# Weights of the stationary-slot products: the low part of every second half built as minus the high part plus the weights, by an accumulating transfer

## The chip, the cores and the metric

One core of one Trainium2 chip runs the whole program. The metric is the device time of one execution, in microseconds (us). Two times stand side by side in the texts: the span of a profiled execution, from its first instruction to its last, and the median of unprofiled runs.

## The reference, cut to what matters

```python
def swiglu(x, w_gate, w_up, w_down):
    return (jax.nn.silu(x @ w_gate) * (x @ w_up)) @ w_down
...
        f = swiglu(rms_norm(h, ffn1_pre_g[i]), ffn1_w_gate[i], ffn1_w_up[i], ffn1_w_down[i])
        h = h + 0.5 * rms_norm(f, ffn1_post_g[i])
        u = rms_norm(h, mix_pre_g[i])
        proj = u @ w_in[i]
...
        merged = g[:, :, 0] * (o_att @ w_branch_att[i]) + g[:, :, 1] * (o_ssm @ w_branch_ssm[i])
        h = h + rms_norm(merged @ w_out[i], mix_post_g[i])
        f = swiglu(rms_norm(h, ffn2_pre_g[i]), ffn2_w_gate[i], ffn2_w_up[i], ffn2_w_down[i])
        h = h + 0.5 * rms_norm(f, ffn2_post_g[i])
```

A decoder layer of width 2048 on 256 tokens in float32: a SwiGLU feed-forward (inner width 5632), then differential attention and a Mamba-2 mixer side by side, then a second feed-forward. Nearly all of the arithmetic is in products of 256 tokens with large float32 weight matrices.

## The kernel before, in words

**Exact products out of two parts.** A float32 number is split into a high part, rounded to the short float32r format (`hi`), and the rest (`lo`). A large product is the sum of hi\*hi, hi\*lo and lo\*hi, gathered in PSUM by TensorE. The tokens' side stands on chip as "slots", already split. The weights stream through the chip once, and every piece is split on arrival.

**Two forms of product.** `project_t` (lines 162 to 177) makes its result [feature, token], with the weights stationary. `project` (lines 121 to 149) makes it [token, feature], with the slots stationary and the weights moving. The change touches `project` alone. It serves the down projections of both feed-forwards (88 chunks), the v, z and gate columns of `w_in` (80), `w_ssm` (32), `w_att` (16) and `w_out` (16): 232 chunks of 1 MB, [128, 4, 512] in float32.

**How one chunk goes through `project`.** SyncE (SP) loads it into a buffer `raw`, of which there are 3 (line 131). It is worked off in two halves of [128, 2, 512]. For each half `split` (lines 102 to 113) takes a `hi` and a `lo` tile out of rings of 4 each, ScalarE (ACT) writes `hi` (line 111) and VectorE (DVE) writes `lo` = `raw` - `hi` (line 112). TensorE (PE) then runs 12 matmuls of 512 columns on the half: for each of two blocks and two token tiles one with `hi` (line 117), one with `lo` (line 118), and one with `hi` again (line 119). A half's `hi` and `lo` go back to their rings when its matmuls are done, and the half four places on takes them. Both kinds of product share the rings.

**Late chunks.** With `by_token=2` (three products: the last slab of each feed-forward and of `w_out`) the last two chunks are held and gone through once per token tile, so four halves stand in the rings at once.

**What sets the order.** Each engine works through its own instructions in one fixed order; a scheduler sets it when the program is built. GpSimd (POOL) does the elementwise multiplications behind `project_t` (lines 304, 306, 386), the decay matrices of the Mamba-2 groups (a DMA into `dec` at line 503, and after DVE's line 505 and ACT's line 507 a multiplication at line 512), small powers (lines 95, 274), and issues a few DMAs. It touches no weights. A list `queue` puts the first splits of a product behind chosen instructions; each call of `split` takes one entry of it.

Of the kernel before, what the change touches and what calls it, by code (L numbers as in the profile page):

```python
"""Macaron SwiGLU pair around differential attention and a Mamba-2 mixer, on one core.

The operand x of a large product stands on chip as "slots" [feature, token], 512 features each. A
float32 operand is the exact sum of two float32r parts (hi = rounded to 12 significant bits, lo =
the rest), and a large product is hi*hi + hi*lo + lo*hi accumulated in PSUM. Weights stream through
SBUF once. A product comes out as [token, feature] (slots stationary, `project`) or, where its
transpose is what is needed next, as [feature, token] (weights stationary, `project_t`).
"""
# [9 lines left out]
F32 = mybir.dt.float32  # L18
F32R = mybir.dt.float32r
AF = mybir.ActivationFunctionType  # L20
ALU = mybir.AluOpType
# [5 lines left out]
NT = 2  # token tiles  # L27
S = 512  # columns of a slab
# [4 lines left out]
# columns of the packed per-partition vectors  # L33
# [3 lines left out]
# slabs of w_in, and of its columns that come out transposed  # L37
# [5 lines left out]
def decoder_layer(ctx: ExitStack, tc: tile.TileContext, x, x_t, cols, rows, post_g, wg1, wu1, wd1, w_in,  # L43
# [15 lines left out]
    # ---- constants  # L59
    ident = const.tile([P, P], F32, name="ident")  # L60
    make_identity(nc, ident)
    tri = const.tile([P, P], F32, name="tri")  # 1 where row <= column
# [3 lines left out]
    neg = const.tile([P, P], F32, name="neg")  # 0 where column <= row, else -1e30  # L66
# [11 lines left out]
    raw0 = raws.tile([P, 8, 256], F32, name="raw")  # the first weights, between the pieces of x  # L78
# [4 lines left out]
    row = const.tile([P, 192], F32, name="row")  # dt_bias | a_log | d, on every partition  # L83
    nc.gpsimd.dma_start(row, rows.partition_broadcast(P))

    def bc(ap, n):
        """[P, k] -> [P, k, n], each element repeated n times."""
        return ap.unsqueeze(2).broadcast_to([P, ap.shape[1], n])

    def rsqrt(dst, ss, n):  # L90
        """dst = (ss / n + eps) ** -0.5"""
        k = ss.shape[1]
        v = small.tile([P, 2], F32, name="rs_v")
        nc.vector.tensor_scalar(v[:, :k], ss, 1.0 / n, EPS, ALU.mult, ALU.add)
        nc.gpsimd.tensor_tensor(out=dst, in0=v[:, :k], in1=mhalf[:, :k], op=ALU.pow)

    loaded = [None]
    queue = []  # instructions that the next splits are issued behind
# [15 lines left out]

    def matmul3(ps, sl, j, t, wh, wl, first, last):
        xh, xl = (sl[:, j, i, t * P:(t + 1) * P] for i in range(2))
        nc.tensor.matmul(ps, xh, wh, start=first, stop=False)  # L117
        nc.tensor.matmul(ps, xh, wl, start=False, stop=False)  # L118
        nc.tensor.matmul(ps, xl, wh, start=False, stop=last)  # L119

    def project(xs, w, n, by_token=0):
        """xs: slots over the contraction; w(n, c): [P, 4, S], the chunk of slot c. -> PSUM [P, NT, S].
        by_token: the last so many chunks are taken token tile by token tile, to have the first of
        them early. -> two PSUM tiles [P, S]."""
        ps = ([psm.tile([P, S], F32, name="acc_t", tag="m") for _ in range(NT)] if by_token else
              acc.tile([P, NT, S], F32, name="acc"))
        at = lambda t: ps[t] if by_token else ps[:, t]
        tail = []
        for c, sl in enumerate(xs):
            raw = raws.tile([P, 4, S], F32, name="raw")  # L130
            nc.sync.dma_start(raw, w(n, c))
            for b in range(2):
                hi, lo = split(raw[:, 2 * b:2 * b + 2], [P, 2, S])
                for jj in range(2):
                    j = 2 * b + jj
                    tail.append((sl, j, hi[:, jj], lo[:, jj], c + j == 0, c == len(xs) - 1 and j == 3))
            if c < len(xs) - by_token:
                for sl_, j, wh, wl, first, last in tail:
                    for t in range(NT):
                        matmul3(at(t), sl_, j, t, wh, wl, first, last)  # L140
                tail = []
        for t in range(NT):
            for sl_, j, wh, wl, first, last in tail:
                matmul3(at(t), sl_, j, t, wh, wl, first, last)
        return ps
# [17 lines left out]
    def project_t(xs, *products, raw=None, before=None):  # L163
        """products: (w, n) each, chunk by chunk in turn; w(n, c): [P, 8, 256], the chunk of slots 2c and
        2c + 1. -> SBUF [feature, 2, token] of each. raw: the first chunk, loaded already;
        before(b, js): what makes the blocks js of slot b."""
        ps = [acc.tile([P, 2, 2 * TT], F32, name="acc") for _ in products]  # hi*hi | hi*lo + lo*hi
        for c in range(len(xs) // 2):
            for i, (w, n) in enumerate(products):
                first = i == 0 and c == 0  # L170
                chunk_t(ps[i], xs, w, n, c, raw if first else None, before if i == 0 else None)
        out = []
        for p in ps:
            out.append(tmp.tile([P, 2, TT], F32, name="pt", tag="t2"))
            nc.scalar.activation(out[-1], p[:, :, TT:], AF.Copy)  # L175
            nc.vector.tensor_tensor(out=out[-1], in0=p[:, :, :TT], in1=out[-1], op=ALU.add)  # L176
        return out
# [4 lines left out]
    def fill(sl, j, src):  # L182
        """Parts of src [P, k, TT] into the slot's blocks j, j + 1, ..."""
        js = slice(j, j + src.shape[1])
        nc.scalar.activation(sl[:, js, 0], src, AF.Copy)
        nc.vector.tensor_tensor(out=sl[:, js, 1], in0=src, in1=sl[:, js, 0].bitcast(F32), op=ALU.subtract)

    def fill_gain(sl, j0, src, gain):
        """The same of src times gain, which has a column for each block of the slot."""
# [7 lines left out]
    def to_slot(src, gain=None):  # L197
        """src: two [P, S] tiles by token -> slot, times gain [P, 4] by feature."""
# [13 lines left out]
    def pre_slots(gain, update):  # L212
        """Slots of h * gain; update(c) brings piece c of h's second token tile up to date."""
        xs = []
        for c in range(4):
            u = update(c)
            if c == 0:
                queue.extend([(), (), (u,), (u,)])
            xs.append(to_slot([h[t][:, c * S:(c + 1) * S] for t in range(NT)], col[:, gain + 4 * c:gain + 4 * c + 4]))
        return xs  # L220

    def pre_scale():
        """The tokens' 1/rms of h, to be applied to the products: [P, NT] by token, and [P, TT] along
        the free axis."""
# [9 lines left out]
    def spread(s1):  # L234
        """Sums of squares by token, [P, NT] -> the pair that pre_scale gives."""
# [11 lines left out]
    class PostNorm:  # L247
        """h += scale * rms_norm(f) * g, f given slab by slab."""
# [6 lines left out]
        def slab(self, n, get):  # L255
# [7 lines left out]
            if n == 2:  # k * (sum of squares / D + eps), but for the last slab's squares  # L263
# [4 lines left out]
        def finish(self):  # L268
            """Brings h of the first token tile up to date. -> what does so for piece c of the second."""
# [64 lines left out]
    # ======== FFN 1  # L334
    xs = [new_slot() for _ in range(4)]

    def scale1():
        """pre_scale of x, from its transpose."""
# [21 lines left out]
    # ======== token mixers  # L360
# [7 lines left out]
    # Work between two products whose steps wait for each other is a generator; one step of it is  # L368
    # issued behind each of the large products.
# [20 lines left out]
    # ---- dt, decays  # L390
# [19 lines left out]
    # softplus(v) = max(v, 0) + 2 atanh(e / (2 + e)), e = exp(-|v|)  # L410
# [10 lines left out]
    nc.vector.tensor_tensor(out=e, in0=e, in1=q, op=ALU.mult)  # z, at most 1/3  # L421
    nc.vector.tensor_tensor(out=q, in0=e, in1=e, op=ALU.mult)  # z * z
# [11 lines left out]
    acs = const.tile([P, NT, 64], F32, name="acs")  # cumulated in each chunk (= token tile)  # L434
# [3 lines left out]
    dend = const.tile([P, 64], F32, name="dend")  # exp(last - acs), first chunk  # L438
    nc.vector.tensor_tensor(out=dend, in0=ptot, in1=acs[:, 0], op=ALU.subtract)
    nc.scalar.activation(dend, dend, AF.Exp)  # L440
    din = const.tile([P, 64], F32, name="din")  # exp(acs), second chunk
# [10 lines left out]
    # ---- lambda  # L452
# [15 lines left out]
    def conv_silu(halves, blocks):  # L468
        """halves: w_in_t slabs; blocks: the conv's 128-channel block of each quarter.
        -> silu(conv) as [channel, block, token]."""  # L470
# [15 lines left out]
    def ssd_group(g, xc, bct, zs):  # L486
        """One group's 8 heads: 512 channels. Appends its slot to done."""
# [3 lines left out]
        xv = hpool.tile([P, 4, S], F32, name="xv", tag="h")  # x*dt of both chunks, x*D of both  # L491
# [7 lines left out]
        # decay between positions of a chunk, [s, head, l]  # L499
# [30 lines left out]
        # the first chunk's state, seen by the second  # L530
# [10 lines left out]
        # gate and group norm  # L541
# [11 lines left out]
    part = big.tile([P, NT, D], F32, name="part", tag="big")  # the ssm branch, then the merge  # L553
# [34 lines left out]
    # ---- attention, two heads a slab  # L588
# [20 lines left out]
    def softmax_av(qT, kT, vs, wait):  # L609
        o, pr, dT = [], {}, {}  # L610

        def probs(hh):
            """Difference of the two maps' softmax, by query."""
# [97 lines left out]
    # ======== FFN 2  # L711
# [54 lines left out]
```

## Time and profile before

| | |
|---|---|
| median of 3 runs | 2865.27 us (2863.51 to 2866.38) |
| span of the profiled execution | 2861.1 us |
| instructions | 36115 |
| bytes moved by DMA | 537.44 MB, 188 GB/s on average |
| granted TensorE clock, mean | 0.997 of full speed (2.4 GHz) |

The profiled execution has no device time of its own beside its span; the median of the runs lies 4.2 us above the span. The busy shares of the engines are averages over the whole program. What decides in a stage is which wait ends last there, so the order of the views is: busy shares, then the chain of waits that ended last, then the instructions of one stage in order of time.

### The profile page before, as it was taken

How to read it: one execution, taken by the hardware profiler on the slowest of the kernel's cores; microseconds unless marked ns; L12 is line 12 of the kernel's file. 1: busy time of each engine (PE TensorE's matmuls, PEld its weight loads, DVE VectorE, ACT ScalarE, POOL GpSimd, SP SyncE). 2: the span in 40 equal slices, each digit the busy share in tenths (PEclk: the TensorE clock that was granted, in tenths of full speed). 3: DMA queues.
4: the chain of work that ended last, by engine and by line, in shares of the span. 5: the costliest groups of instructions: out<-in, count | busy, mean ns of one | idle time of the engine just before them, and what ended most of it. 6: DMA issues, size and time to landing. Idle time of an engine off the chain costs nothing.

```text
span 2861.1 us, 36115 instructions
## 1 busy us (share of the span) xinstructions
PE 2823.8 (99%) x14540; PEld 2398.2 (84%) x14540; DVE 1707.9 (60%) x2018; ACT 1374.3 (48%) x1695; POOL 285.8 (10%) x219
## 2 busy tenths in 40 slices
PE   8999999999999999999999999999999999999998
PEld 7888888888788888888788888888878888888887
DVE  6554555555678776777765555545556545554555
ACT  5444444444555555545444444444455444443443
POOL 1100110011012210112100000000001100110110
PEclk9999999999999999999999999999999999999999
DMA  6565555556554555545554545555545555555554
GB/s 238 188 219 190 186 190 191 192 186 200 192 198 168 179 189 179 189 162 192 205 182 171 177 167 185 199 191 184 195 171 180 191 192 189 191 183 197 183 195 155
DMA packets 77127, 537.44 MB, mean 188 GB/s; under 512 B 8672, under 2 KB 8816, under 8 KB 13728
## 3 DMA queue, kind: packets, MB, share of 16 engines
q1 hardware_dynamic: 73152, 521.17, 53.2%
q0 software_dynamic: 3664, 13.80, 1.5%
q8 instruction: 114, 1.87, 0.3%
q14 instruction: 53, 0.43, 0.0%
q10 hardware_dynamic: 144, 0.17, 0.0%
HBM read 530.84 MB, written 4.26 MB: 187 GB/s over the span
## 4 chain that ended last, share of the span: by engine, by line
PE 91%; issue 4%; DVE 3%; DMA 0%; ACT 0%; POOL 0%; SPq 0%; DVEq 0%; POOLq 0%; ACTq 0%
PE acc L159 33%; PE acc L160 17%; PE acc L118 13%; PE acc L119 13%; PE acc L117 13%; PE pyd L525 1%; DVE w_lo L112 1%; PE tp L205 1%; PE sc L618 0%; PE po L646 0%; DVE dec L505 0%; DVE xc L480 0%; DMA xT<-in_x_t 0%; PE pyo L537 0%; PE pst L532 0%
## 5 line engine op out<-in xcount | busy, mean ns | idle before, releaser
L112 DVE TENSOR_TENSOR w_lo<-raw,w_hi 128x1024 fp32r<-128x1024 f32 (+1 forms) x979 | 1245.8, 1276 | 1028.9 <-ACT w_hi L111 1026.7
L111 ACT ACTIVATE w_hi<-raw 128x1024 fp32r<-128x1024 f32 (+1 forms) x979 | 1034.5, 1059 | 1249.5 <-PE acc L159 631.1
L159 PE MATMUL acc<-slot,w_hi 128*128 128x512 f32 x4096 | 1448.8, 399 | 8.5 <-DVE slot L193 7.1
L160 PE MATMUL acc<-slot,w_lo 128*128 128x256 f32 x4096 | 1148.5, 280 | 0.5 <-DVE w_lo L112 0.5
L159 PEld LDWEIGHTS acc<-slot,w_hi 128*128 128x128 f32 x4096 | 770.3, 188 | 194.4 <-ACT w_hi L111 9.5
L160 PEld LDWEIGHTS acc<-slot,w_lo 128*128 128x128 f32 x4096 | 774.2, 189 | 4.0 <-DVE w_lo L112 2.3
L118 PE MATMUL acc<-w_lo,slot 128*128 128x512 f32 x1776 | 693.3, 390 | 6.0 <-DVE w_lo L112 6.0
L117 PE MATMUL acc<-w_hi,slot 128*128 128x512 f32 x1776 | 697.4, 393 | 0.0
L119 PE MATMUL acc<-w_hi,slot 128*128 128x512 f32 x1776 | 692.8, 390 | 0.0
L118 PEld LDWEIGHTS acc<-w_lo,slot 128*128 128x128 f32 x1776 | 334.2, 188 | 77.2 <-DVE w_lo L112 7.2
L117 PEld LDWEIGHTS acc<-w_hi,slot 128*128 128x128 f32 x1776 | 334.3, 188 | 70.5 <-issue 1.0
L119 PEld LDWEIGHTS acc<-w_hi,slot 128*128 128x128 f32 x1776 | 334.1, 188 | 69.3
L304 POOL TENSOR_TENSOR pt<-pt,rb 128x512 f32<-128x512 f32 x44 | 58.9, 1338 | 1118.4 <-DVE pt L176 1113.6
L176 DVE TENSOR_TENSOR pt<-acc,pt 128x512 f32<-128x512 f32 x128 | 87.5, 683 | 2.6 <-ACT pt L175 2.6
L175 ACT ACTIVATE pt<-acc 128x512 f32<-128x512 f32 x128 | 74.3, 580 | 1.8 <-PE acc L160 1.8
L480 DVE SCALAR_TENSOR_TENSOR xc<-pt,col,xc 128x255 f32<-128x255 f32 (+2 forms) x144 | 61.9, 482 | 14.1 <-ACT xc L477 13.9
L306 POOL TENSOR_TENSOR pt<-pt,rb 128x512 f32<-128x512 f32 x44 | 65.2, 1483 | 33.7 <-ACT pt L305 33.7
L512 POOL TENSOR_TENSOR dec<-dec,cb 128x1024 f32<-128x1024 f32 x16 | 55.8, 3504 | 121.9 <-ACT dec L507 121.9
L386 POOL TENSOR_TENSOR pt<-pt,rb 128x512 f32<-128x512 f32 x24 | 36.5, 1521 | 208.7 <-DVE pt L176 208.7
L477 ACT ACTIVATE xc<-pt,col 128x256 f32<-128x256 f32 x48 | 26.8, 594 | 40.3 <-POOL pt L386 40.3
L305 ACT ACTIVATE pt<-pt 128x512 f32<-128x512 f32 x44 | 27.9, 633 | 26.1 <-POOL pt L304 26.1
L309 DVE TENSOR_TENSOR pt<-pt 128x512 f32<-128x512 f32 x44 | 30.5, 692 | 7.5 <-POOL pt L306 3.1
(195 smaller groups left out, 1034.8 us busy)
## 6 DMA issues: line engine op xcount, KB each, us to landing
raw<-in_wu SPq DMA_DIRECT2D x88, 1024.0 KB, 4.8
raw<-in_wd SPq DMA_DIRECT2D x88, 1024.0 KB, 4.9
raw<-in_wg SPq DMA_DIRECT2D x87, 1024.0 KB, 4.9
raw<-in_w_in SPq DMA_DIRECT2D x80, 1024.0 KB, 4.8
raw<-in_w_in_t SPq DMA_DIRECT2D x80, 1024.0 KB, 4.9
raw<-in_w_ssm SPq DMA_DIRECT2D x32, 1024.0 KB, 4.8
raw<-in_w_att SPq DMA_DIRECT2D x16, 1024.0 KB, 4.8
raw<-in_w_out SPq DMA_DIRECT2D x16, 1024.0 KB, 4.8
```

Source lines behind the costliest of these rows:

```text
L111: nc.scalar.activation(hi[:, js], raw[:, js], AF.Copy)
L112: nc.vector.tensor_tensor(out=lo[:, js], in0=raw[:, js], in1=hi[:, js].bitcast(F32), op=ALU.subtract)
L117: nc.tensor.matmul(ps, xh, wh, start=first, stop=False)
L118: nc.tensor.matmul(ps, xh, wl, start=False, stop=False)
L119: nc.tensor.matmul(ps, xl, wh, start=False, stop=last)
L159: nc.tensor.matmul(ps[:, f], hi[:, j, wf], sl[:, j], start=b + j == 0, stop=False)
L160: nc.tensor.matmul(ps[:, f, TT:], lo[:, j, wf], sl[:, j, :TT], start=False, stop=b == len(xs) - 1 and j == 3)
L175: nc.scalar.activation(out[-1], p[:, :, TT:], AF.Copy)
L176: nc.vector.tensor_tensor(out=out[-1], in0=p[:, :, :TT], in1=out[-1], op=ALU.add)
L304: nc.gpsimd.tensor_tensor(out=g, in0=g, in1=rb, op=ALU.mult)
L306: nc.gpsimd.tensor_tensor(out=g, in0=g, in1=rb, op=ALU.mult)
L480: nc.vector.scalar_tensor_tensor(out=xc[:, j, d:], in0=v[:, k, :TT - d], scalar=w(3 - d), in1=xc[:, j, d:], op0=ALU.mult, op1=ALU.add)
```

## The change

The first half of each chunk in `project` is split as before. For the second half a new function, `split_dma`, has ACT write `hi` and then `lo` = -`hi`, and POOL issue a transfer that reads the half's weights from DRAM once more and adds them onto `lo`. DVE has no part in it. Comments and docstrings are gone too, and every line behind the new function stands 10 to 13 lines lower.

```diff
+    def split_dma(raw, src):
...
+        hi = wsplit.tile([P, 2, S], F32R, name="w_hi", tag="whi")
+        lo = wsplit.tile([P, 2, S], F32R, name="w_lo", tag="wlo")
+        nc.scalar.activation(hi, raw, AF.Copy)
+        nc.scalar.activation(lo, hi.bitcast(F32), AF.Copy, scale=-1.0)
+        nc.gpsimd.dma_start(lo, src, accum_op=ALU.add)
+        return hi, lo
...
             for b in range(2):
-                hi, lo = split(raw[:, 2 * b:2 * b + 2], [P, 2, S])
+                if b:
+                    hi, lo = split_dma(raw[:, 2:4], w(n, c)[:, 2:4])
+                else:
+                    hi, lo = split(raw[:, 0:2], [P, 2, S])
```

Two places show what this does to the order. The first is ACT in the first down projection (`f<-acc` drains the product's PSUM). Before:

```order
L111 ACTIVATE w_hi<-raw 128x1024 x6
L323 ACTIVATE f<-acc 128x2x512
L111 ACTIVATE w_hi<-raw 128x1024 x8
L323 ACTIVATE f<-acc 128x2x512
L111 ACTIVATE w_hi<-raw 128x1024 x8
L323 ACTIVATE f<-acc 128x2x512
```

A product of four chunks was eight writes of `hi` in a row, then the drain. The same place in the changed kernel:

```order
L336 ACTIVATE f<-acc 128x2x512
L120 ACTIVATE w_hi<-raw 128x1024
L121 ACTIVATE w_lo<-w_hi 128x1024
L111 ACTIVATE w_hi<-raw 128x1024
L120 ACTIVATE w_hi<-raw 128x1024
L121 ACTIVATE w_lo<-w_hi 128x1024
L111 ACTIVATE w_hi<-raw 128x1024
L120 ACTIVATE w_hi<-raw 128x1024
L121 ACTIVATE w_lo<-w_hi 128x1024
L111 ACTIVATE w_hi<-raw 128x1024
```

Each chunk now has three writes on ACT instead of two, and the drain stands ahead of the `hi` and `lo` of a second half.

The second place is POOL around the first branch of `w_ssm` products (behind Mamba-2 group 3; `pt<-pt,rb` is the multiplication behind `project_t`, `ssm_r` a small power). Before:

```order
L386 TENSOR_TENSOR pt<-pt,rb 128x512 x2
L503 DMA dec<-acsD 128x1024 x2
L95 TENSOR_TENSOR ssm_r<-rs_v,mhalf 128x2
L512 TENSOR_TENSOR dec<-dec,cb 128x1024 x2
L95 TENSOR_TENSOR ssm_r<-rs_v,mhalf 128x2
L386 TENSOR_TENSOR pt<-pt,rb 128x512 x4
```

In the changed kernel:

```order
L399 TENSOR_TENSOR pt<-pt,rb 128x512
L122 DMA w_lo<-in_w_in 128x1024 x2
L399 TENSOR_TENSOR pt<-pt,rb 128x512
L122 DMA w_lo<-in_w_in 128x1024 x2
L122 DMA w_lo<-in_w_ssm 128x1024
L516 DMA dec<-acsD 128x1024 x2
L122 DMA w_lo<-in_w_ssm 128x1024
L95 TENSOR_TENSOR ssm_r<-rs_v,mhalf 128x2
L525 TENSOR_TENSOR dec<-dec,cb 128x1024 x2
L122 DMA w_lo<-in_w_ssm 128x1024 x6
L95 TENSOR_TENSOR ssm_r<-rs_v,mhalf 128x2
L399 TENSOR_TENSOR pt<-pt,rb 128x512 x3
```

The transfers onto `lo` stand in POOL's row between its own work: six of the eight that the `w_ssm` products need come behind the two multiplications of `dec`.

## Rows read from the trace of the kernel before

**Rows 1.** The page: span, then busy time, share, instructions of each engine.
```profile
span 2861.1 us, 36115 instructions
...
PE 2823.8 (99%) x14540; PEld 2398.2 (84%) x14540; DVE 1707.9 (60%) x2018; ACT 1374.3 (48%) x1695; POOL 285.8 (10%) x219
```

**Rows 2.** The page: chain that ended last, by engine and by line.
```profile
PE 91%; issue 4%; DVE 3%; DMA 0%; ACT 0%; POOL 0%; SPq 0%; DVEq 0%; POOLq 0%; ACTq 0%
PE acc L159 33%; PE acc L160 17%; PE acc L118 13%; PE acc L119 13%; PE acc L117 13%; PE pyd L525 1%; DVE w_lo L112 1%; PE tp L205 1%; PE sc L618 0%; PE po L646 0%; DVE dec L505 0%; DVE xc L480 0%; DMA xT<-in_x_t 0%; PE pyo L537 0%; PE pst L532 0%
```

**Rows 3.** Timeline, a down projection of FFN 1: start, duration, instruction, idle before.
```profile
241.42 0.39 PE L119 MATMUL acc<-w_hi,slot 128*128 128x512 f32 x1
241.64 0.39 PE L117 MATMUL acc<-w_hi,slot 128*128 128x512 f32 x1
...
241.84 1.06 ACT L111 ACTIVATE w_hi<-raw 128x1024 fp32r<-128x1024 f32 x1 [1.66 <-PE acc L119]
...
242.94 1.23 DVE L112 TENSOR_TENSOR w_lo<-raw,w_hi 128x1024 fp32r<-128x1024 f32 x1 [1.49 <-ACT w_hi L111]
...
244.19 11.21 SPq L131 DMA_DIRECT2D raw<-in_wd  x3
244.36 0.39 PE L117 MATMUL acc<-w_hi,slot 128*128 128x512 f32 x1
...
249.80 0.39 PE L117 MATMUL acc<-w_hi,slot 128*128 128x512 f32 x1
...
250.03 0.39 PE L118 MATMUL acc<-w_lo,slot 128*128 128x512 f32 x1
```

**Rows 4.** Groups by line and form: busy us, mean ns, idle before and releaser.
```profile
L112 DVE TENSOR_TENSOR w_lo<-raw,w_hi 128x1024 fp32r<-128x1024 f32 x977 | 1244.4, 1277 | 1025.9 <-ACT w_hi L111 1023.8
L111 ACT ACTIVATE w_hi<-raw 128x1024 fp32r<-128x1024 f32 x977 | 1033.3, 1059 | 1246.5 <-PE acc L159 631.1 <-PE acc L119 578.3 <-issue 9.6
```

**Rows 5.** Waits: who waited for whom, us in total, times, longest.
```profile
ACT w_hi L111 <- PE acc L119: 578.3, 367, 2.2
```

**Rows 6.** DMA issues: KB each, median us from issue to landing.
```profile
raw<-in_wd SPq DMA_DIRECT2D x88, 1024.0 KB, 4.9
...
dec<-acsD POOLq DMA_DIRECT2D x16, 512.0 KB, 5.3
```

**Rows 7.** The line of the dec transfers, L503: issue ns, and landing.
```profile
L503 POOL DMA_DIRECT2D dec<-acsD x16: 544/563/683, 840.7 to 1365.1; - x16
...
DMA to landing us min/median/max: 3.9/5.3/6.1
```

**Rows 8.** The line of the two 1 MB transfers that POOL issues, L705.
```profile
L705 POOL DMA_DIRECT2D hb<-hsave x2: 547/574/601, 1415.8 to 1416.4; - x2
...
DMA to landing us min/median/max: 6.9/7.8/8.8
```

**Rows 9.** Stretches: length, busy of PE, PEld, DVE, ACT, POOL, clock, DMA share, GB/s.
```profile
216.00:255.00 39.00, 39.00 (x173) 32.28 (x172) 18.34 (x15) 16.38 (x16) 0.00 (x0) 1.00 0.56 189
...
1418.00:1422.00 4.00, 4.00 (x25) 3.51 (x24) 1.23 (x1) 1.30 (x2) 0.00 (x0) 1.00 1.00 422
```

**Rows 10.** Timeline, first w_ssm branch: POOL, then PE.
```profile
1046.27 2.52 POOL L512 TENSOR_TENSOR dec<-dec,cb 128x1024 f32<-128x1024 f32 x1 [3.27 <-ACT dec L507]
1050.24 4.38 POOL L512 TENSOR_TENSOR dec<-dec,cb 128x1024 f32<-128x1024 f32 x1 [1.45 <-ACT dec L507]
...
1053.89 0.39 PE L118 MATMUL acc<-w_lo,slot 128*128 128x512 f32 x1
```

**Rows 11.** Groups by line and form: ACT's drains of PSUM behind project.
```profile
L571 ACT ACTIVATE zs<-acc,pre_rstd 128x512 f32<-128x512 f32 x16 | 10.2, 680 | 6.6 <-PE acc L119 6.6
L677 ACT ACTIVATE gate<-acc,pre_rstd 128x512 f32<-128x512 f32 x16 | 10.1, 686 | 10.0 <-PE acc L119 10.0
...
L323 ACT ACTIVATE f<-acc 128x1024 f32<-128x1024 f32 x8 | 8.2, 1028 | 13.3 <-PE acc L119 13.3
...
L605 ACT ACTIVATE v<-acc,pre_rstd 128x512 f32<-128x512 f32 x8 | 5.1, 684 | 6.6 <-PE acc L119 6.6
...
L560 ACT ACTIVATE part<-acc 128x1024 f32<-128x1024 f32 x4 | 4.1, 1026 | 5.3 <-PE acc L119 5.3
```

## The prediction

> **What bounds the kernel now.** I read the busy shares first. PE is busy for 2823.8 of 2861.1 us, 99%, while DVE has 60% and ACT 48% [rows 1]. So at most 37.3 us can be won by anything that leaves PE its work. The chain of waits says the same: 91% of it is PE's matmuls, and DVE has 3% [rows 2]. DVE's 1244.4 us on `lo` are its largest group [rows 4], but they lie beside PE. The change takes work from an engine that is not the bound, so the question is what it costs.
>
> Then I read one stage in order of time, a down projection in steady state [rows 3]. PE's matmuls start 0.227 us apart: from 241.64, the first of a half, to 244.36, the first of the next, is 2.72 us for 12. ACT writes a `hi` at 241.84, right after PE's last matmul of a half (241.42 + 0.39 = 241.81). It had waited for PE, and not for the load: over the program 578.3 us of such waits stand against line 119 [rows 5]. **So the rings of four halves set the pace of the splits**: a half's parts can only be begun when the half four places before it is finished. DVE then writes `lo` from 242.94 to 244.17. PE wants that half three halves later, with its first matmul at 249.80 (241.64 + 3 x 2.72) and the first `lo` at 250.03. DVE's way thus has 5.6 us to spare. This spare time is what the change spends.
>
> **The change part by part.** *Removed:* 232 subtractions on DVE of 1.277 us [rows 4], 296 us, all in the shade of PE: worth 0 us. *Added on ACT:* 232 copies with scale -1, at the 1.059 us of the copy of that size [rows 4], 246 us. ACT goes from 48% to about 57%; per chunk it has 3 x 1.06 = 3.2 of 5.44 us, so it does not become the bound. *Added on POOL:* 232 issues at 0.563 us [rows 7], 131 us on an engine that is busy for 10%.
>
> *Added for the DMA engines:* 232 x 0.52 MB = 122 MB from DRAM a second time, and the adder must read `lo` as well. A stage at 5.44 us a chunk has its engines busy 56% of the time at 189 GB/s, and the fastest stretch reached 422 GB/s [rows 9]. With 1.05 MB loaded and 1.05 MB read for the sum, 2.1 MB in 5.44 us are 385 GB/s. That stays under 422, so rate alone does not stop PE. But transfers will queue: SP frees `raw` once the last reader is done (244.19 behind DVE's end at 244.17 [rows 3]). That reader is now ACT, so each 1 MB load starts about 1.1 us ahead of each accumulation and shares its engines. The loads have room: three buffers, and a landing of 4.9 us [rows 6] with about 6 us to spare.
>
> *The new path of a second half*, from the same rows [rows 3]: `hi` starts at 241.84, two ACT copies take 2.12, and two hand-overs take 0.04 each (242.90 to 242.94), so POOL can issue at 244.04. I let PE need the sum at 249.81, when the `lo` matmul's slot is loaded. **The transfer has 5.8 us from issue to landing.** Any excess e stops PE. The half that was stopped frees its tiles e later for the half four places on, which is two chunks; both chains of second halves share the stop, so each chunk grows by e/2.
>
> *How long does it take to land?* No accumulating transfer is in the trace. The nearest row from below is `dec`, also 512 KB issued by POOL: 5.3 us, between 3.9 and 6.1 [rows 7]. From above: the two 1 MB transfers that POOL issued back to back beside loads, 6.9 and 8.8 us [rows 8]. The sum reads 512 KB of weights and 512 KB of `lo`, 1 MB as they do, and writes half. 512 KB at 422 GB/s are 1.24 us; `dec` is then 4.06 + 1.24, and two readings make 6.5, in good agreement with 6.9. I take 6.9. If the adder ran at a quarter of the copy's rate, the same formula gives 4.06 + 4 x 1.24 = 9.0. The ends are 5.3 and 9.0.
>
> That an add in a DMA engine costs a second read is also what the Trainium skill says in "Collectives: The Full Stack", under "The bandwidth ceiling: the fold count and why AG ≠ RS ≠ AR": the addition itself is free, but two source reads share one read ring. No run here shows it yet; by it the sum stands, and with one read it is that of the first rival.
>
> *Terms of the sum.*
> 1. Steady state: e = 6.9 - 5.8 = 1.1, half of it for each of 232 chunks: 128 us.
> 2. POOL's order. At the first `w_ssm` branch the transfer of the second product's first chunk stands behind the `dec` multiplications, which wait for ACT and end at 1050.24 + 4.38 = 1054.62. With 6.9 us it lands at 1061.5, while PE used that `lo` at 1053.89 [rows 10]: 7.6 us. The other two branches have the same order: 23 us. Behind `project_t` a transfer meets one multiplication, and DMAs ahead of it are issued first; I cost that at 0, as it is done before the ring has let the next one go.
> 3. The three `by_token` products run four resident halves at 6 x 0.227 = 1.36 us each. Their last half's tile comes free when the pass begins (t = 0), so its sum lands at 2.2 + 6.9 = 9.1; the second half's lands at 9.1 - 5.44 = 3.7, where PE wants it at 1.36 + 0.23 = 1.6 (2.1 late); the last is then wanted at 4.3 + 2.1 = 6.4 (2.7 late). 4.8 us each, 14 us.
> 4. ACT's drains now stand ahead of a second half's copies, with no spare time behind them. They are 10.2 + 10.1 + 8.2 + 5.1 + 4.1 = 37.7 us [rows 11]; where one chain is late the other has slack, so I take half, 19 us.
> 5. The entries of `queue` at the mixers' start now fall on other halves, once in the program: 0, and at most one landing (6.9 us) either way.
>
> 128 + 23 + 14 + 19 = 184 us. The span goes from 2861.1 to 3045, and a median of runs, 4.2 us above as it was, to **3049 us, 6.4% slower**.
>
> **The rivals.** *The sum lands inside its room.* If adding costs no more than copying (5.3 us), term 1 is 0. Term 2 is 3 x (1054.62 + 5.3 - 1053.89) = 18, term 3 is 3 x (0.5 + 2.7) = 10, and term 4 some 10, as half a microsecond of spare remains: 38 us, 2903. For it: the 3.9 of the fastest `dec`; against it: the second read, the load that starts just before, and 6.1 for the slowest. The Trainium skill speaks for it, in "DMA: Bandwidth & Descriptors", under "Anatomy of one DMA — SWDGE (gpsimd) path": about 2.0 us and the bytes at 436 GB/s, an estimate of 3.2 us for 512 KB. The trace disagrees for a copy beside loads: 5.3 [rows 6].
>
> *The adder is slow.* At 9.0 us term 1 is 1.6 x 232 = 371, term 2 is 29, term 3 is 3 x (3.7 + 3.2) = 21, term 4 stays: 440 us, 3305; each further microsecond adds 116. For it: no row shows the adder, and 1.05 us of engine time per chunk separates 385 from 422 GB/s only if a read is all it costs. Then the engines saturate, and the loads come late too.
>
> *Faster.* DVE gets 296 us back, and where its queue held up a `lo` PE stood still: that is the 1% of the chain put down to line 112 [rows 2], at most some 29 us, down to 2836. It decides only where every sum lands within 5.8 us and POOL holds none back, against term 2, which follows from POOL's order alone. Half of those waits are in first halves, which stay on DVE.
>
> That the change does not do what it says, with no transfer issued, is excluded by POOL's row, which has them.
>
> **How the numbers follow.** A measurement of this kernel can tell about 0.2%, some 6 us, from no change. Chances: my forecast (a landing between about 6.2 and 8.2 us, 2970 to 3210) 0.52; inside its room 0.24; slow adder 0.20; faster 0.04, of which over 0.2% 0.03. Of "inside its room" 0.04 goes to within 0.2%, since all its terms may hide; with the rest of "faster" that makes 0.05. Slower: 0.92. The range reaches from the first rival, 2890, to 3400, a landing of 9.8 us; what is left out is faster or the same (0.08) and a slower adder still (0.10).
>
> **What would show it.** The transfers onto `lo` at line 122, 232 of them, landing in about 6.9 us. PE waiting for them at line 128 (the matmul with `lo`) once in each chunk, some 0.5 us on average, in total about 130 to 180 us; PE's busy share near 93%. DVE's group on `lo` with 747 instead of 979 entries. Long waits of 7 to 8 us at the three `w_ssm` branches. I am wrong if PE's waits for `lo` are rare (landing under 5.8), if they reach 1.5 us a chunk (the adder), or if PE waits for `raw`.

## The result, and the profile after

| | before | changed |
|---|---|---|
| time, median of 4 runs each | 2865.82 us (2863.51 to 2866.79) | 3146.38 us (3138.27 to 3160.05) |
| profiled execution: own time / span | as shown ahead | 3160.05 / 3158.3 us |

The change is **9.88% slower: ratio 1.0988, 95% interval [1.0966, 1.1011]**. The forecast was 6.4% (3049 us). Its sign, its mechanism and its range (2890 to 3400) held; the size was some 100 us short. The profiled execution was the slowest of its four runs, 14 us above their median, so sums from its trace stand to a difference of 297 us between the spans, not of 281.

The page of the changed kernel, parts 1, 3, 4, 5 and 6 (groups are: line, engine, operation, count | busy us, mean ns | idle before, and its releaser):

```profile
span 3158.3 us, 36605 instructions
...
PE 2906.0 (92%) x14540; PEld 2399.5 (76%) x14540; DVE 1438.0 (46%) x1786; ACT 1609.9 (51%) x1927; POOL 479.7 (15%) x451
...
q1 hardware_dynamic: 73152, 521.17, 48.5%
q0 software_dynamic: 37072, 135.45, 22.8%
...
PE 30%; DMA 16%; ACT 4%; issue 1%; DVE 0%; POOL 0%; DVEq 0%; POOLq 0%
...
L112 DVE TENSOR_TENSOR w_lo<-raw,w_hi 128x1024 fp32r<-128x1024 f32 (+1 forms) x747 | 955.9, 1282 | 1474.4 <-ACT w_hi L111 1473.1
...
L128 PE MATMUL acc<-w_lo,slot 128*128 128x512 f32 x1776 | 723.0, 407 | 202.4 <-DMA w_lo<-in_wd 83.0
...
L121 ACT ACTIVATE w_lo<-w_hi 128x1024 fp32r<-128x1024 f32 x232 | 245.8, 1059 | 6.0
...
raw<-in_wd SPq DMA_DIRECT2D x88, 1024.0 KB, 6.5
...
w_lo<-in_wd POOLq DMA_DIRECT2D x88, 512.0 KB, 7.8
```

Against [rows 1], DVE lost 270 us of work, and the kernel got slower. In the chain DMA stands at 16%, where it had 0% [rows 2]. PE still does 14540 matmuls, but stood still for 202 us ahead of the `lo` matmuls of line 128 (line 118 before), and what ended most of that was a transfer. The loads land later too: 6.5 us for `wd`, where it was 4.9 [rows 6].

The line of the transfers (issue ns min/median/max; landing us):

```profile
L122 POOL DMA_DIRECT2D w_lo<-in_wd x88: 852/862/909, 191.5 to 3137.3; - x88
...
DMA to landing us min/median/max: 5.6/7.8/10.3
```

The median is 7.8 us, where 6.9 was taken. An issue costs POOL 0.86 us, where the plain one took 0.563 [rows 7].

The stage of [rows 3] in the timeline of the changed kernel, one engine after the other:

```profile
240.31 0.50 PE L128 MATMUL acc<-w_lo,slot 128*128 128x512 f32 x1 [1.36 <-DMA w_lo<-in_wd]
...
247.46 0.50 PE L128 MATMUL acc<-w_lo,slot 128*128 128x512 f32 x1 [1.41 <-DMA w_lo<-in_wd]
247.80 0.40 PE L129 MATMUL acc<-w_hi,slot 128*128 128x512 f32 x1
...
254.55 0.50 PE L128 MATMUL acc<-w_lo,slot 128*128 128x512 f32 x1 [1.32 <-DMA w_lo<-in_wd]
...
243.14 1.06 ACT L120 ACTIVATE w_hi<-raw 128x1024 fp32r<-128x1024 f32 x1 [3.32 <-PE acc L129]
...
244.23 1.06 ACT L121 ACTIVATE w_lo<-w_hi 128x1024 fp32r<-128x1024 f32 x1
...
245.58 0.86 POOL L122 DMA_DIRECT2D w_lo<-in_wd  x1 [6.24 <-ACT w_lo L121]
```

Here is the loop that was forecast: PE frees a half, ACT writes `hi` and `-hi`, POOL issues, PE stops for the sum. The stops are 7.1 us apart, (254.55 - 240.31) / 2, where a chunk took 5.44. ACT ends at 245.29 and POOL issues at 245.58: a hand-over of 0.29, where 0.04 was taken.

The DMA view of the same stretch, 216 to 255 us, and its windows (columns as in [rows 9]):

```profile
raw<-in_wd SPq DMA_DIRECT2D x6, 1024.0 KB, 7.8
...
w_lo<-in_wd POOLq DMA_DIRECT2D x6, 512.0 KB, 8.9
```

```profile
216.00:255.00 39.00, 30.90 (x130) 23.59 (x129) 6.76 (x6) 19.45 (x19) 5.17 (x6) 1.00 0.87 221
539.40:542.80 3.40, 3.40 (x10) 2.66 (x9) 1.13 (x1) 1.10 (x2) 0.00 (x0) 0.50 0.58 119
1150.40:1157.20 6.80, 4.90 (x12) 3.85 (x13) 1.23 (x1) 1.42 (x2) 0.87 (x1) 0.50 0.96 260
```

In steady state the sum takes 8.9 us and the load 7.8. The rule of the ring, half of (landing + later hand-over - room) a chunk, gives (8.9 + 0.3 - 5.8) / 2 = 1.7 us; 7.1 - 5.44 is 1.7. The engines' share rose from 0.56 to 0.87 [rows 9], while the rate rose only from 189 to 221 GB/s: their time goes into something that the bytes don't count.

The other two stretches show what nobody had costed. The first begins behind a stop of PE of 2.0 us, the second in one of 3.9, and the granted clock is 0.50 in them, the 1.2 GHz level. Over the program, without its start and end, such stretches make 64.8 us, 16 of them, against 13.7 us in 3 before; 14 of the 16 begin in or behind single stops of 1.8 to 4.8 us.

### The profile page after: what moved, and what is told of

It is laid out like the page before. It is cut to its first block, busy times and chain, and to the rows that moved or that the text cites. A ratio compares the mean times of both kernels' runs of the same rounds, so it can differ in the third digit from the quotient of the medians.

```text
span 3158.3 us, 36605 instructions
## 1 busy us (share of the span) xinstructions
PE 2906.0 (92%) x14540; PEld 2399.5 (76%) x14540; DVE 1438.0 (46%) x1786; ACT 1609.9 (51%) x1927; POOL 479.7 (15%) x451
## 3 DMA queue, kind: packets, MB, share of 16 engines
q1 hardware_dynamic: 73152, 521.17, 48.5%
q0 software_dynamic: 37072, 135.45, 22.8%
## 4 chain that ended last, share of the span: by engine, by line
PE 30%; DMA 16%; ACT 4%; issue 1%; DVE 0%; POOL 0%; DVEq 0%; POOLq 0%
PE acc L172 14%; PE acc L173 7%; DMA w_lo<-in_w_in 6%; DMA w_lo<-in_wd 5%; PE acc L128 3%; PE acc L129 3%; PE acc L127 2%; DMA w_lo<-in_w_att 2%; DMA w_lo<-in_w_out 2%; ACT w_lo L121 2%; ACT w_hi L120 2%; DMA w_lo<-in_w_ssm 1%; PE po L659 0%; PE tp L218 0%; PE sc L631 0%
## 5 line engine op out<-in xcount | busy, mean ns | idle before, releaser
L112 DVE TENSOR_TENSOR w_lo<-raw,w_hi 128x1024 fp32r<-128x1024 f32 (+1 forms) x747 | 955.9, 1282 | 1474.4 <-ACT w_hi L111 1473.1
L111 ACT ACTIVATE w_hi<-raw 128x1024 fp32r<-128x1024 f32 (+1 forms) x747 | 788.6, 1057 | 796.2 <-PE acc L172 589.8
L128 PE MATMUL acc<-w_lo,slot 128*128 128x512 f32 x1776 | 723.0, 407 | 202.4 <-DMA w_lo<-in_wd 83.0
L127 PE MATMUL acc<-w_hi,slot 128*128 128x512 f32 x1776 | 705.3, 397 | 0.0
L129 PE MATMUL acc<-w_hi,slot 128*128 128x512 f32 x1776 | 701.6, 395 | 0.0
L120 ACT ACTIVATE w_hi<-raw 128x1024 fp32r<-128x1024 f32 x232 | 245.8, 1060 | 505.3 <-PE acc L129 452.5
L127 PEld LDWEIGHTS acc<-w_hi,slot 128*128 128x128 f32 x1776 | 338.5, 191 | 75.5 <-issue 1.2
L129 PEld LDWEIGHTS acc<-w_hi,slot 128*128 128x128 f32 x1776 | 338.6, 191 | 65.6
L121 ACT ACTIVATE w_lo<-w_hi 128x1024 fp32r<-128x1024 f32 x232 | 245.8, 1059 | 6.0
L317 POOL TENSOR_TENSOR pt<-pt,rb 128x512 f32<-128x512 f32 x44 | 58.8, 1337 | 791.8 <-DVE pt L189 787.0
L122 POOL DMA_DIRECT2D w_lo<-in_wd x88 | 75.9, 862 | 485.2 <-ACT w_lo L121 451.1
L122 POOL DMA_DIRECT2D w_lo<-in_w_in x80 | 69.9, 874 | 376.8 <-ACT w_lo L121 354.2
L319 POOL TENSOR_TENSOR pt<-pt,rb 128x512 f32<-128x512 f32 x44 | 65.2, 1481 | 33.7 <-ACT pt L318 33.7
```

Of the source, the lines that this page charges most:

```text
L111: nc.scalar.activation(hi[:, js], raw[:, js], AF.Copy)
L112: nc.vector.tensor_tensor(out=lo[:, js], in0=raw[:, js], in1=hi[:, js].bitcast(F32), op=ALU.subtract)
L120: nc.scalar.activation(hi, raw, AF.Copy)
L121: nc.scalar.activation(lo, hi.bitcast(F32), AF.Copy, scale=-1.0)
L122: nc.gpsimd.dma_start(lo, src, accum_op=ALU.add)
```

## The experiments

Ratios are to the kernel before, run on the same chip. "Landing" is the time from a transfer's issue to its landing, at the median where nothing else is said. "Stops" is the time by which PE's start of the first `lo` matmul of a second half lay more than 0.227 us behind the start before it, over the 232 chunks: 6.0 us before, 234.8 us in the changed kernel, 176 of them over 0.2 us. The chunks are counted off by 24 matmuls in PE's order, so in the `by_token` products some stops fall outside the count.

**The transfer as a copy.**

```diff
-        nc.gpsimd.dma_start(lo, src, accum_op=ALU.add)
+        nc.gpsimd.dma_start(lo, src)
```

> The transfer onto lo is a plain copy of the same weights from DRAM, without the addition (so lo holds the weights and not the rest); ACT's copy to lo, POOL's issues and the order stay. My theory, that the sum is late because adding needs a second read in the DMA engines: the landing falls from 7.8 us to about 5.5 (the 5.3 of the dec transfers), e = 5.5 + 0.3 - 5.8 = 0, the stops at the second halves' lo fall from 235 us to under 40, and the time to 2880 to 2920 us. Rival, that any transfer in this place is late (POOL's issue, packets, the load beside it): the landing stays above 7 us and the time above 3050.

2963.69 us, ratio 1.0332 [1.0314, 1.0350]; stops 69.4 us. The page, and the transfer's line:

```profile
q0 software_dynamic: 37072, 135.45, 13.9%
```

```profile
L122 POOL DMA_DIRECT2D w_lo<-in_wd x88: 527/527/601, 191.7 to 2943.6; - x88
...
DMA to landing us min/median/max: 3.8/5.6/8.2
```

The landing falls by 2.2 us and the time by 183 us: **most of the loss is the addition**. Queue 0, which holds the transfers that POOL issues, moves the same 135.45 MB in the same 37072 packets, in 13.9% of 2962.5 us, where it took 22.8% of 3158.3. Without the 13.80 MB that were there before, at 1.5% of 2861.1 us, these are 369 and 677 us of all 16 engines for 121.65 MB: 3.0 us a megabyte as a copy (a load takes 2.9: 48.5% of 3158.3 us for 521.17 MB), and 5.6 as a sum. The ratio is 1.8. The Trainium skill, in "Collectives: The Full Stack", "The bandwidth ceiling: the fold count and why AG ≠ RS ≠ AR", puts the cost of an add at its two source reads, with a measured ratio of 1.93 for collectives. The ratio here comes near that; no run separates the reads from the adding. The expected time was 44 to 84 us too low: a copy misses its 5.8 us too, with landings up to 8.2, and each miss has the side costs described below.

**Half of the second halves.** In a chunk of even number both halves are split on DVE as before; 112 transfers remain.

```diff
-                if b:
+                if b and c % 2:
```

> Only the chunks with an odd number have their second half made by an accumulating transfer: 116 transfers in place of 232. My theory, a ring of four halves whose stop is shared by two chains, says that half as many transfers stop PE nearly as long: each waits its whole e = 7.5 + 0.3 - 5.8 = 2.0 us instead of half of it, 116 x 2.0 = 232, less what is saved because the DMA engines are freer: 3030 to 3110 us, and a stop per transfer near 1.7 us instead of 1.0. Rival, that each transfer costs the same on its own (1.0 us): 116 x 1.2 = 140, 3000 us, and with the engines as the bound (rate): half of the added bytes, under 2950.

3066.62 us, ratio 1.0698 [1.0677, 1.0720]; landing 7.0 at the median; stops 155.5 us, 94 over 0.2 us. Half of the transfers keep 71% of the loss. If each stop were paid alone, half of it would stay; here only one of the two chains of second halves is late, so the whole e is paid per transfer: 7.0 + 0.3 - 5.8 = 1.5 against 155.5 / 112 = 1.4. With all of them it is e/2, 234.8 / 232 = 1.0. That is the ring, as forecast.

**No transfer.** `lo` is `-hi`; only the DMA line is gone.

> The transfer is left out: lo of a second half is only minus hi. What is left of the change is ACT's second copy, the relief of DVE, and the new order on ACT. My theory puts these at 0 to 20 us: 2860 to 2890. Rival, that ACT's longer row (its drains ahead of a second half's copies) carries a good part of the loss: above 2930. If DVE's relief is worth something, below 2860.

2860.62 us, ratio 0.9980 [0.9970, 0.9989]; stops 0.0. ACT's third write per chunk, its new order and what DVE is spared make together 0.2% less; the run does not tell them apart. So everything that the change costs hangs on the transfer.

**A shorter path:** `lo` is made from `raw` first, then the transfer, then `hi`.

```diff
-        nc.scalar.activation(hi, raw, AF.Copy)
-        nc.scalar.activation(lo, hi.bitcast(F32), AF.Copy, scale=-1.0)
+        nc.scalar.activation(lo, raw, AF.Copy, scale=-1.0)
         nc.gpsimd.dma_start(lo, src, accum_op=ALU.add)
+        nc.scalar.activation(hi, raw, AF.Copy)
```

> ACT writes lo = -round(raw) straight from the weights, POOL issues the transfer, and only then ACT writes hi: the path from a freed tile to the issue is one ACT copy (1.06 us) shorter, the rest is as in the change. By the ring, 1.06 us of path is worth half of it in each of 232 chunks: 123 us less where every chunk is stopped; 176 of 232 are, so 93 to 123 us less: 3025 to 3055 us. Rival, that the rate of the DMA engines sets the pace: the landing grows by what the path loses, and the time stays within 30 us of 3146.

3091.27 us, ratio 1.0780 [1.0761, 1.0799]; stops 162.1 us. The transfer starts 1.06 us earlier and the run is 55 us shorter, where 93 to 123 were expected. Stops fell by 73 us; the landing rose from 7.8 to 8.0, and the stretches at 0.50 from 64.8 to 78.5 us. Room is worth what the ring says, less what the later landing takes back: half of 1.06 - 0.2, 176 times, is 76 us.

**The second operand from the chip:** the transfer reads `raw` in place of DRAM.

```diff
-        nc.gpsimd.dma_start(lo, src, accum_op=ALU.add)
+        nc.gpsimd.dma_start(lo, raw, accum_op=ALU.add)
```

> The addition reads the weights from the raw buffer on chip and not from DRAM again. Both readings remain, but raw is let go only when the sum has landed, so the next 1 MB load no longer starts just ahead of the transfer. My theory (two readings, and the load that shares the engines): the landing falls from 7.8 to about 6.2 us, e = 6.2 + 0.3 - 5.8 = 0.7, half of it in 232 chunks 81 us, and 2950 to 3000 us in all. Rival, that the second reading of DRAM is what is slow: a landing near 5.5 and under 2920. Rival, that the adder alone is the time: a landing still above 7.3 and above 3080; or the loads, held back, become the wait: waits for raw, above 3100.

3114.94 us, ratio 1.0891 [1.0859, 1.0924]: a miss. The landing on the page is even shorter than the 6.2 expected; the waits (who waited for whom, us, times, longest) and the timeline do not follow it:

```profile
q0 software_dynamic: 37072, 135.45, 22.6%
...
w_lo<-raw POOLq DMA_DIRECT2D x232, 512.0 KB, 5.5
```

```profile
PE acc L128 <- DMA w_lo<-raw: 152.6, 93, 3.4
...
ACT w_hi L111 <- DMA raw<-in_wd: 35.5, 22, 3.0
```

```profile
235.23 0.79 PE L128 MATMUL acc<-w_lo,slot 128*128 128x512 f32 x1 [3.36 <-DMA w_lo<-raw]
...
236.25 0.63 PE L127 MATMUL acc<-w_hi,slot 128*128 128x512 f32 x1
236.67 0.63 PE L128 MATMUL acc<-w_lo,slot 128*128 128x512 f32 x1
```

Stops are 173.8 us in 97: half as many as in the changed kernel, and 1.8 us long instead of 1.3. After one of 3.36 us matmuls start 0.42 us apart instead of 0.227: the clock. Stretches at 0.50 make 143 us. ACT waits for loads too, since the transfer now holds `raw` until it lands. For the engines it hardly matters where the second operand lies: 22.6% of 3110.2 us are 5.4 us a megabyte, reckoned as above.

**The load sent behind the transfer.** SP sends 64 bytes of each sum to DRAM, and the load three chunks on comes behind that.

```diff
+                    scraps.append(nc.sync.dma_start(scrap, lo[0:1, 0, 0:16].bitcast(F32)))
...
-            nc.sync.dma_start(raw, w(n, c))
+            with tc.issue_after(scraps[-3].ins) if len(scraps) > 2 else nullcontext():
+                nc.sync.dma_start(raw, w(n, c))
```

> As the change, but SP sends 64 bytes of each sum to a scrap buffer ahead of the load three chunks on, so that load waits until the sum has landed: the transfer from DRAM has the engines to itself. My theory: the landing falls from 7.8 to 5.8 to 6.5 us, stops of 60 to 110 us, 2940 to 3010 us. Rival, that the load beside it does not matter: landing above 7.3 and above 3090. If the loads then come late, waits for raw show in ACT's rows and the time rises over 3146.

3218.26 us, ratio 1.1235 [1.1218, 1.1251]: a miss, slower than the change. Its landing, its waits and its clock:

```profile
DMA to landing us min/median/max: 5.4/6.3/11.4
```

```profile
ACT w_hi L113 <- DMA raw<-in_wd: 57.4, 34, 4.3
```

```profile
core 0: 3220.2 us, clock 0.965
```

The median landing falls to 6.3, but the load then comes late, the stops are 251.4 us in only 100, and 218 us run at a clock of 0.50. Nor does the edit part the two. Of the 232 sums, 93 still have a load issued between 2 us before them and 1 us after: they land in 8.1, and 81 of them stop PE. The other 139 land in 5.8, and 21 of those stop it.

**From `raw`, with four load buffers** (the kernel above with `raws` at 4 and, for the room, `tmp` at 8), and two controls.

> The addition reads from the raw buffer on chip, as in the run before with that, now with 4 raw buffers in place of 3 (four temporaries fewer make the space), so that a load held back until the sum has landed is no longer late. There the landing had fallen to 5.5 us, but ACT waited 165 us for loads. If the late loads were what kept the time up: 2920 to 2980 us. If the time stays above 3080, the late loads were not it, and the rare long landings (to 11 us) are.

3103.73 us, ratio 1.0839 [1.0809, 1.0868]. ACT's waits for `raw` are down from 140.6 us (not the 165 of the expectation) to 3, and the time hardly moves: late loads were not the reason. Stops are 164.2 us in 95. At a stop, issue to PE's use is 7.4 us at the median, against a landing of 5.6 over all.

Which sums are late can be read from the trace of the run that reads `raw` with three load buffers. The timeline, then the DMA views of the issues from 225.5 to 226.5 us and from 221 to 222:

```profile
225.97 0.86 POOL L122 DMA_DIRECT2D w_lo<-raw  x1 [3.67 <-ACT w_lo L121]
...
226.08 0.33 SPq L141 DMA_DIRECT2D raw<-in_wd  x1
```

```profile
raw<-in_wd SPq DMA_DIRECT2D x1, 1024.0 KB, 6.6
w_lo<-raw POOLq DMA_DIRECT2D x1, 512.0 KB, 9.2
```

```profile
w_lo<-raw POOLq DMA_DIRECT2D x1, 512.0 KB, 4.5
```

The sum issued at 221.44 starts 3.7 us behind the last load and lands in 4.5. With that it lets its `raw` go, and the next load starts at 226.08, together with the next sum. That one takes 9.2 us, and it is the one that PE stood still for above, 3.36 us. Over the whole run, 82 sums have a load issued between 2 us before them and 1 us after. They land in 7.7, and 76 of them stop PE; the other 150 land in 5.2, and 24 of those stop it. With four load buffers it is 87 sums in 7.6 against 145 in 5.1, in the changed kernel 205 in 7.9 against 27 in 6.1. So most late sums are late by a load that starts beside them, and reading from `raw` leaves this to every third sum or so; how the engines share between the two queues no view shows.

> The kernel before with two temporaries fewer, as the run with lo ahead has them: what this alone costs. 2860 to 2880 us; above 2900 the run with lo ahead would have to be read against it.

2863.84 us, ratio 0.9999 [0.9990, 1.0008].

> The change itself with 4 raw buffers and four temporaries fewer: control for the run above. By my theory the loads were not late in the change and the rings are as they were: 3120 to 3170 us, landing 7.8. A gain of over 60 us would say that loads did hold it back.

The changed kernel with four load buffers: 3142.38 us, ratio 1.0972 [1.0954, 1.0991]; stops 226.9 us. Neither fewer scratch buffers nor, together with them, a fourth load buffer make a difference that can be told from noise.

**The transfer started a chunk ahead.** The second halves' `lo` gets a ring of three of its own (first halves keep two; `tmp` has 10), and is begun as soon as its load is there.

```diff
+        stage(0)
+        for c, sl in enumerate(xs):
+            if c + 1 < len(xs):
+                stage(c + 1)
```

> The second halves' lo get a ring of their own with 3 tiles (the first halves' 2), and ACT writes lo = -round(raw) one chunk ahead, so a sum has two halves (5.4 us) more to land; two temporaries fewer make the space. Bytes, adder and loads are those of the change. My theory, that the landing is late against the ring and that the engines' rate is not the bound: stops at second halves under 25 us in all, 2870 to 2905 us. Rival, that the engines cannot move the bytes in 5.44 us a chunk: still above 3000 us, with landings that grow over 10 us.

2890.47 us, ratio 1.0100 [1.0072, 1.0129]. It also has one `lo` tile more, and makes `lo` from `raw` as the shorter path does. The transfer's line, and the window of the down projection:

```profile
DMA to landing us min/median/max: 5.5/8.9/14.4
```

```profile
216.00:255.00 39.00, 39.00 (x174) 32.31 (x173) 8.58 (x7) 22.59 (x23) 6.03 (x7) 1.00 1.01 277
```

This settles the bound. The sums of the same bytes land **later** than in the changed kernel, at 8.9 and up to 14.4 us, the engines are full (1.01, 277 GB/s), and PE is busy for 39.00 of 39.00 us. Stops are 7.6 us. Neither the adder's rate nor that of the engines stops PE: the time from a tile's release to its use does.

**Five halves in the ring,** for the changed kernel and for the one before (`tmp` 8):

```diff
-    wsplit = E(name="wsplit", bufs=4)
+    wsplit = E(name="wsplit", bufs=5)
```

> The change with one more tile in each ring (5 in place of 4) and four temporaries fewer, and nothing else: a sum has one half, 2.72 us, more, 8.5 us from issue to landing. With the landing of 7.8 to 8.9 us, e is at most 0.7 and mostly under 0: stops of 20 to 70 us, 2885 to 2950 us. Rival, the rate of the DMA engines: landings grow with the room, and it stays above 3050.

2960.27 us, ratio 1.0328 [1.0302, 1.0355], landing 8.4. One more half gives back two thirds of the loss; stops are 77.8 us. It lies 10 us above what was expected; the longest single wait is at a `w_ssm` product, behind POOL:

```profile
PE acc L128 <- DMA w_lo<-in_w_ssm: 18.9, 5, 8.0
```

> The kernel before with rings of 5 and four temporaries fewer: whether the longer rings alone win anything, as PE's few waits for lo there (6 us) may. 2855 to 2866 us.

**2849.34 us, ratio 0.9947 [0.9933, 0.9961]: half a per cent below the kernel before, with an interval clear of 1.** PE's longest waits in it:

```profile
PE acc L159 <- ACT w_hi L111: 6.9, 1, 6.9
PE tp L205 <- DVE h L282: 2.2, 1, 2.2
PE acc L160 <- DVE w_lo L112: 1.8, 2, 1.3
```

PE's stops for `lo` at line 118, 6.0 us in the kernel before, are down to 0.1, and the stretches at 0.50 from 13.7 to 3.4 us. The span is 12.3 us shorter. This is better than expected (2855 to 2866). The run also has four scratch buffers fewer; two fewer alone changed nothing (2863.84 us), four fewer alone were not run.

## Why the prediction was right in kind and short in size

- **The bound, and what DVE's relief is worth.** Right. PE set the pace, and sparing DVE 232 subtractions is worth 0.2%, net of what ACT's copies cost (no transfer).
- **ACT's copies, POOL's issues, the rate of the engines.** Costed at nothing: right for ACT by the same run, and for the rate by the run with the transfer a chunk ahead, but with nothing to spare: the engines' share is 1.01 there, at 277 GB/s and not at the 422 of [rows 9]. POOL's hand-over (0.29 instead of 0.04) takes 0.25 us more of the path; its issue (0.86 instead of 0.563) lies inside the landing.
- **The ring and e/2.** Right, and shown three ways: 1.7 us against 1.7 in the down projection, 1.4 against 1.5 with every other transfer, and the stops gone with 2890 us when the transfer leaves the ring.
- **The step that failed: the size of term 1, "I take 6.9".** It landed in 7.8 at the median and 8.9 in the steady down projection. The 6.9 was the faster of two 1 MB copies, with 6.5 from a copy's formula with a second reading beside it. What the runs showed in its place: a copy itself, in this place, takes 5.6, the addition 2.2 more; and a load and a sum that start together slow each other. The 205 sums with a load so near land in 7.9, the other 27 in 6.1, and the loads take 6.5 and 7.8 instead of 4.9. The prediction named this load, 1.1 us ahead of each sum, and gave it no price. The bound of 9.0, taken for a "slow adder", is what a steady stretch has.
- **Term 2, POOL's order: too big.** 23 us forecast, 11 measured (3.9, 4.0 and 3.1). The order was as described:

```profile
1143.38 3.23 POOL L525 TENSOR_TENSOR dec<-dec,cb 128x1024 f32<-128x1024 f32 x1 [1.45 <-ACT dec L520]
1146.56 0.90 POOL L122 DMA_DIRECT2D w_lo<-in_w_ssm  x1
```

  PE's stop for that sum ended at 1152.30, after 3.86 us. So the transfer took 5.7 us rather than 6.9, and PE wanted it at 1148.4, 1.8 us behind the multiplication, where the forecast had 0.7 us ahead of it: PE was itself late by then. The step had kept PE on the old schedule.
- **Term 3, the `by_token` products.** 14 us forecast; the waits for `lo` at line 128 into `acc_t` are 6.9 + 6.8 = 13.7 (15 when counted like the stops, from start to start).
- **Term 4, the drains.** It can't be told apart from term 1. Stops are 229 us above before's 6.0. Of these 11 are term 2's and 4 term 3's, so 214 stand against 128 + 19 = 147.
- **Missing: what a stop costs besides its length.** The spans differ by 297 us. 229 are the stops counted, and 13 are stops for `lo` outside the count, 11 of them term 3's. Some 56 are neither. Of these at most 26 are the clock: 51 us more at half of it, in which PE does half the work. Behind each stop the second matmul starts 0.34 us after the first (247.46 and 247.80), 0.11 more than in steady state: about 20 us over 176 stops. A single wait of `project_t` for a `lo` of DVE, at 1084.58, is 3.7. The rest, some 6 us, stays unassigned.

By these the sum is 184 + 67 (terms 1 and 4) - 12 (term 2) + 1 (term 3) + 1 (other first halves) + 56 = 297.

Two figures of the slow-adder rival do not come out of its rows. Moving 2.1 MB at 422 GB/s takes 4.97 us, so 0.47 us a chunk separates 385 from 422 GB/s, not 1.05. And at 9.0 us term 3 is 4.2 + 2.7 a product, not 3.7 + 3.2; their sum is the same.

The signs that were named: 232 transfers, 747 entries on DVE, PE at 92% for 93%, as stated; 202 us of waits at line 128 in place of 130 to 180; 3 to 4 us at the `w_ssm` branches in place of 7 to 8. The rival with the landing inside its room has little support: 5.6 was the fastest, and with the later hand-over that just fills the room. By the Trainium skill's figures in "DMA: Bandwidth & Descriptors", "Anatomy of one DMA — SWDGE (gpsimd) path", the estimate for 512 KB was 3.2 us. The copy took 5.6 here at the median and 3.8 at the least, so the measurement decides.

## What to carry to other kernels

In a ring of buffers, don't weigh an engine's busy time but the room from a buffer's release to its next use: work off the bound is free only as long as its latency, with hand-overs, fits in there. A transfer that starts on the same event as a larger one is to be costed at a landing beside that one, not at the median of the whole program. If the room is short, a deeper ring or an earlier start can give as much as a faster transfer or more: one more half in the ring lost 3.3% at a landing of 8.4 us, as the plain copy did at 5.6, and the transfer a chunk ahead lost 1.0% at 8.9.

## What the runs showed of the hardware

- **An accumulating transfer** took 5.6 us of all 16 DMA engines a megabyte, a plain copy of the same packets 3.0, and its issue took POOL 0.86 us instead of 0.53. With the second operand on chip it was 5.4.
- **TensorE's clock follows the stops, the long ones above all.** Behind stops the granted clock was 0.50 (1.2 GHz) for a while. The time at 0.50 was 64.8 us in the changed kernel (176 stops, 1.3 us each), 143 us reading from `raw` (97, 1.8 us), 218 us with the load behind (100, 2.5 us): in these three runs fewer and longer stops cost more of it. With no stops (no transfer) it was 17 us, and with five halves in the ring of before 3.4 us.
- **A load that starts beside a transfer makes it late.** Sums with a 1 MB load issued between 2 us before them and 1 us after landed in 7.9 us in the changed kernel, 7.7 reading from `raw` and 8.1 with the load behind; the others of the same runs in 6.1, 5.2 and 5.8.
- **A shorter median landing need not be a shorter time.** Two edits brought it down to 5.5 and 6.3 us and lost 8.9% and 12.4%: the median mixed sums that met a load with sums that did not, and 76 and 81 of those that met one stopped PE. Late loads are excluded as the reason for the first; how the engines share between queues was not shown.
